# Layer 0's attention in pieces, with the order of four engines written out for seven heads

## The chip, the cores and the metric

The kernel runs on one core of a Trainium2 chip. The core has a matmul engine (PE, TensorE), a vector engine (DVE, VectorE), an activation engine (ACT, ScalarE), a general engine (POOL, GpSimd) and a queue that issues transfers (SP, SyncE). Each engine works through its own list of instructions in order and waits on semaphores of the others. The metric is the device time of one execution in microseconds (us), lower is better; the time before is the median of three runs.

## The reference

A trunk of two layers on 1024 positions of 1024 values in float32. Layer 0 mixes positions by differential attention, layer 1 by latent attention, and each is followed by a gated feed-forward block with a causal convolution. The change touches layer 0's attention: 8 heads, each with two score maps on 64 dimensions and one value map of 128.

```
q, k, v = split(h @ w_qkv)               # q, k: 8 heads x 2 maps x 64;  v: 8 heads x 128
q, k = rope on the first 16 of each 64
lam = exp(sum(lq1*lk1)) - exp(sum(lq2*lk2)) + lambda_init
sc = q k^T / 8                           # per head and map, keys up to the query's chunk of 64
p = softmax(sc)
a = p[map 0] - lam * p[map 1]
o = rms_norm(a @ v, subln_g) * (1 - lambda_init)
x = x + o @ w_o
```

## The kernel before

**Tiling.** Matrix products run in a reduced float32 format; to keep precision every operand is split into a high part (`hi`, a ScalarE cast) and a remainder (`lo`, a subtraction), and `mm3` (L116) issues three matmuls for a product, at lines 119 to 121. A head needs six projection units of 24 matmuls of 512 columns: keys, queries and values, for the first and the second half of the positions. They accumulate in a single PSUM bank, named `u`. A value sum is copied (L556) and then transposed; a key or query sum goes through a swap (L237) and a cosine product (L238) on VectorE, then two steps on GpSimd (L239, L240), then casts and remainders. The next unit can't start in bank `u` before its reader has finished.

**Steps.** `steps` (L281) runs 32 steps, t = 4 x head + p. Step p takes the query blocks 2p and 2p+1 (j = 0, 1; 128 rows each) against all keys up to their own. For each j: scores of both maps (L1622, L1623) into one of two double banks `S` (one holds both maps for p = 0 and 1, for p = 2 and 3 each map has its own), the mask and the maximum (L1626 to L1631), two exponentials with their sums (L1637), the reciprocal (L1647), the factor with lambda (L1648), the scaling of map 0 (`scale`: GpSimd L149 for p = 0 and 1, ScalarE L147 for p = 2 and 3) and the mix of the two maps (L1650). One step later the mixed weights are transposed in groups of up to four blocks of 128 (L252), split (`hi`, `lo`) and multiplied with the values; the product of 256 columns is copied (L1665). Every second step closes half a head's output: squares (L1668, L1669, remainder on GpSimd), their sum by two matmuls with ones (L1678, L1679), the root (`rsqrt`, L170) and a store by SP. Three banks `b` rotate among transposes, products and sums.

**Weights.** A head's three weight tiles are fetched by SP into two places in turn, split by ScalarE (1024 columns, `hi`) and GpSimd (`lo`, 1024 columns), and kept in four tiles. `prepare` (L515) does one split a step and fetches the next tile.

**What sets the order.** Before the steps a stretch is written out by hand (`manual_schedule`). The steps themselves are left to the framework's scheduler, which orders each engine by its own estimate of when things are ready; `steps` only gives it the program order: scores 0, projection piece, transposes of the step before, scaling and scores 1, the other projection pieces, products of the step before. Tiles that share a place make the later writer wait for the earlier readers.

## Time and profile before

| | us |
|---|---|
| median of 3 runs | 2427.79 (2427.32 to 2431.45) |
| profiled execution | 2430.68 |
| its span | 2428.9 |
| first scores of head 0 (from the span's start) | 48.12 |
| first scores of head 7 | 459.04 |

The profile shows one execution. Busy time is what an engine's instructions took; the idle time before an instruction is put down to the one that released it. In a row of instructions, "out<-in" names the tiles: `u<-s,s` on PE is a projection into bank u, `S<-u,h` and `S<-u,u` are scores, `b<-ident,u` transposes of the weights, `b<-u,u` products with the values. Casts are often printed at line 127 and remainders at line 130, the lines of `hi` and `lo`. DVE's idle time counts only where someone waits for DVE.

### The profile page before, as it was taken

The page shows a single profiled execution, that of the slowest core. Times are in us where ns is not written, and L with a number is a line of the kernel's source. Part 1 is how long each engine was busy: PE and PEld are TensorE (multiplying, and loading weights), DVE is VectorE, ACT ScalarE, POOL GpSimd, SP SyncE. Part 2 cuts the span into 40 slices and gives each one's busy share as a digit, 9 for nine tenths or more (in the row PEclk, how much of TensorE's full clock was granted, in tenths as well). Part 3 has the DMA queues.
Part 4 walks back from the last instruction along what each step waited for, and adds up shares of the span by engine and source line. Part 5 has one row for each costly group of instructions (what it writes and reads, how often), then busy time and mean ns, then how long its engine had stood idle before and what let it go on. Part 6 is the DMA issues. An engine that isn't in the chain of part 4 may idle for free.

```text
span 2428.9 us, 32660 instructions
## 1 busy us (share of the span) xinstructions
PE 2355.0 (97%) x11936; PEld 1997.5 (82%) x11936; DVE 1916.0 (79%) x3111; ACT 1305.3 (54%) x2446; POOL 618.5 (25%) x489
## 2 busy tenths in 40 slices
PE   7999999999999999999999999999999999999998
PEld 6888787887888888878899788988878888887886
DVE  6667776857888888889964777887488888888997
ACT  5677777755444444444445777776244444444444
POOL 4545454424100000000041666665330000000001
PEclk9999999999999999999999999999999999999999
DMA  4111111223322222554221211114322222227502
GB/s 161 40 35 44 35 35 44 100 93 100 99 82 79 87 78 88 187 175 131 72 103 46 77 40 29 49 59 134 96 87 87 79 87 87 78 86 278 172 3 78
DMA packets 95792, 213.91 MB, mean 88 GB/s; under 512 B 8720, under 2 KB 33936, under 8 KB 95632
## 3 DMA queue, kind: packets, MB, share of 16 engines
q1 hardware_dynamic: 86448, 184.04, 23.1%
q10 hardware_dynamic: 9184, 27.79, 3.1%
q8 instruction: 94, 1.54, 0.3%
q14 instruction: 66, 0.54, 0.1%
HBM read 159.37 MB, written 52.43 MB: 87 GB/s over the span
## 4 chain that ended last, share of the span: by engine, by line
PE 82%; DVE 7%; ACT 5%; DMA 3%; issue 2%; POOL 1%; SPq 0%; DVEq 0%; POOLq 0%; ACTq 0%
PE S L119 13%; PE S L121 13%; PE S L120 13%; PE b L119 8%; PE b L120 8%; PE b L121 8%; PE u L119 4%; PE u L120 4%; PE u L121 4%; PE b L252 3%; DMA u<-g_d 2%; PE u L1727 1%; DVE s L130 1%; PE u L1726 1%; ACT s L127 1%
## 5 line engine op out<-in xcount | busy, mean ns | idle before, releaser
L167 POOL TENSOR_TENSOR st<-st,mhalf 128x1 f32<-128x1 f32 x56 | 36.6, 654 | 1314.1 <-DVE st L164 1305.5
L127 ACT CAST u<-h 128x512 fp32r<-128x512 f32 (+2 forms) x242 | 145.9, 619 | 297.4 <-DVE h L847 277.7
L119 PE MATMUL S<-s,u 128*128 128x512 f32 (+1 forms) x768 | 290.5, 378 | 7.6 <-ACT s L127 2.6
L121 PE MATMUL S<-s,u 128*128 128x512 f32 (+1 forms) x768 | 289.5, 377 | 0.1
L120 PE MATMUL S<-s,u 128*128 128x512 f32 (+1 forms) x768 | 289.4, 377 | 0.0
L119 PE MATMUL b<-s,u 128*128 128x512 f32 x588 | 231.0, 393 | 1.5 <-DVE u L130 0.8
L121 PE MATMUL b<-s,u 128*128 128x512 f32 x588 | 229.3, 390 | 0.0
L120 PE MATMUL b<-s,u 128*128 128x512 f32 x588 | 229.2, 390 | 0.0
L904 DVE SCALAR_TENSOR_TENSOR u<-u,conv,u 128x1023 f32<-128x1023 f32 (+1 forms) x176 | 225.8, 1283 | 1.4 <-ACT u L900 1.4
L149 POOL TENSOR_TENSOR u<-u,st 128x384 f32<-128x384 f32 (+7 forms) x160 | 169.7, 1068 | 151.0 <-DVE st L1712 106.7
L127 ACT CAST s<-u 128x512 fp32r<-128x512 f32 (+2 forms) x230 | 145.0, 666 | 108.2 <-PE u L121 35.8
L119 PE MATMUL u<-s,s 128*128 128x512 f32 (+1 forms) x440 | 178.5, 406 | 13.4 <-ACT h L556 7.0
L130 DVE TENSOR_TENSOR u<-b,u 128x512 fp32r<-128x512 f32 (+1 forms) x256 | 157.4, 629 | 29.4 <-ACT u L127 28.0
L119 PEld LDWEIGHTS S<-s,u 128*128 128x128 f32 x768 | 145.2, 189 | 35.1 <-ACT s L127 5.5
L121 PE MATMUL u<-s,s 128*128 128x512 f32 (+1 forms) x440 | 173.2, 394 | 0.0
L120 PE MATMUL u<-s,s 128*128 128x512 f32 (+1 forms) x440 | 172.8, 393 | 0.0
L121 PEld LDWEIGHTS S<-s,u 128*128 128x128 f32 x768 | 145.2, 189 | 26.6 <-DVE u L130 0.5
L120 PEld LDWEIGHTS S<-s,u 128*128 128x128 f32 x768 | 145.3, 189 | 26.1
L130 DVE TENSOR_TENSOR s<-u,s 128x512 fp32r<-128x512 f32 (+2 forms) x210 | 150.0, 746 | 12.4 <-ACT s L127 12.2
L127 ACT CAST u<-b 128x512 fp32r<-128x512 f32 (+1 forms) x256 | 133.2, 550 | 37.9 <-PE b L252 28.9
L907 ACT ACTIVATE u<-u 128x1024 f32<-128x1024 f32 x44 | 46.7, 1062 | 187.5 <-DVE u L904 187.5
L130 DVE TENSOR_TENSOR u<-h,u 128x512 fp32r<-128x512 f32 x164 | 112.7, 687 | 32.5 <-ACT u L127 31.5
(270 smaller groups left out, 6561.1 us busy)
## 6 DMA issues: line engine op xcount, KB each, us to landing
u<-in_ffn_up SPq DMA_DIRECT2D x88, 512.0 KB, 3.9
g_d<-u ACTq DMA_DIRECT2D x44, 512.0 KB, 2.6
u<-in_ffn_down SPq DMA_DIRECT2D x66, 256.0 KB, 4.8
u<-g_d SPq DMA_DIRECT2D x62, 256.0 KB, 4.4
s<-in_da_wqkv SPq DMA_DIRECT2D x23, 512.0 KB, 3.6
x_d<-u SPq DMA_DIRECT2D x16, 512.0 KB, 2.9
s<-x_d SPq DMA_DIRECT2D x8, 1024.0 KB, 10.8
u<-o_d SPq DMA_DIRECT2D x24, 256.0 KB, 2.9
```

Source lines behind the costliest of these rows:

```text
L119: mm(out, lh, rl, start=first, stop=False, skip_group_check=onto)
L120: mm(out, lh, rh, start=False, stop=False, skip_group_check=onto)
L121: mm(out, ll, rh, start=False, stop=last, skip_group_check=onto)
L127: self.nc.scalar.copy(out, src)
L130: (eng or self.nc.vector).tensor_sub(out, src, hi.bitcast(F32))
L149: self.nc.gpsimd.tensor_mul(x, x, s.to_broadcast(list(x.shape)))
L167: nc.gpsimd.tensor_tensor(r, s, self.mhalf, ALU.pow)
L252: self.nc.tensor.transpose(ps[:, j * P : (j + 1) * P], probs[t][:, k : k + P], self.ident)
L904: nc.vector.scalar_tensor_tensor(t[half][:, back:], u[half][:, : S - back], w, t[half][:, back:], ALU.mult, ALU.add)
L907: nc.scalar.activation(t[0], t[0], AF.Silu)
L1726: nc.tensor.matmul(o[:, c0:], v, al, start=kb == 0, stop=False)
L1727: nc.tensor.matmul(o[:, c0:], v, ah, start=False, stop=kb == 2 * p + 1)
```

## The change

The work of a step is cut into some 45 named pieces, and a table with one row for each p says in which order they are issued, for steps 0 to 27 (heads 0 to 6) on PE, DVE, ACT and POOL (`da_steps`). A name without a mark belongs to the step itself, each `'` to one step earlier, `+` to the next. The letters: S scores, M mask and maximum, E exponential, I reciprocal and lambda product, C scaling, X mix, T transposes, H high part, L remainder, A product with the values, O its copy, Q squares, F their sum, R and N the root on ScalarE and VectorE, Wh and Wl the split of a weight tile. U and V are the step's projection units: 0 and 1 are the halves of its 24 matmuls, c the copy, t the transposes, h and l the split of values, s the swap, m the cosine, p and a the two GpSimd steps, ka to kd and qa to qf the casts and remainders of keys and queries. Head 7 keeps the old manner, with the same pieces called in a fixed sequence and then ordered by the scheduler.

```diff
+    DA_SCORE = (
+        "S0 S1 M0 Up O'' R2''' V0 X1' R3''' N1''' M1 T1' Ua E0a H1' L1' Uka E1a T0' H0' T2' Ukb Ukc V1 E0b L0' I0 E1b A0' N2''' T3'",
...
+    def da_steps(self, attend, units, prepare, n):
+        E = mybir.EngineType
+        region = ExitStack()
+        region.enter_context(self.tc.manual_schedule(engines={E.PE, E.DVE, E.Activation, E.Pool}))
+        steps, last = [], 28
+        for t in range(-1, n + 2):
...
+            if t == last:
+                region.close()
...
+            for name in self.DA_SCORE[t % 4].split():
+                step = t - name.count("'") + name.count("+")
+                if 0 <= step < min(n, last):
+                    steps[step](name.strip("+'"))
+            if t < last:
+                continue
...
```

A weight tile's fetch is now issued with the remainder that frees its place:

```diff
         def split_w(h, which):
...
+            def high():
+                st.raw = raws.pop((h, which))
+                st.w = self.w([P, 2, D], F32R)
+                heads[h]["w", which] = st.w[:, 0, :], st.w[:, 1, :]
+                self.hi(st.w[:, 0, :], st.raw)
+
+            def low():
+                self.lo(st.w[:, 1, :], st.raw, st.w[:, 0, :], nc.gpsimd)
+                fetch_w(*{1: (h, 2), 0: (h + 1, 1), 2: (h + 1, 0)}[which])
```

The lambda product moves from ScalarE to VectorE, and the root reads the sum's bank directly; its sign is turned, and the gain's with it:

```diff
-        nc.scalar.mul(w, l[:, 1:2], k.neglam)
+    def invert(self, j):
+        k.nc.vector.reciprocal(l, l)
+        k.nc.vector.tensor_scalar_mul(l[:, 1:2], l[:, 1:2], k.neglam)
...
-        nc.scalar.activation(v, x, AF.Identity, bias=self.eps, scale=scale)
-        nc.scalar.activation(t, v, AF.Ln)
+            act(self.tmp, self.ss, AF.Ln, bias=k.eps, scale=1.0 / P)
...
-        nc.vector.scalar_tensor_tensor(t, t, -0.5, v, ALU.mult, ALU.mult)
-        nc.vector.scalar_tensor_tensor(r, t, 1.5, r, ALU.add, ALU.mult)
+            stt(self.tmp, self.ss, EPS * P, self.tmp, ALU.add, ALU.mult)
+            stt(self.r, self.tmp, 1.5, self.r, ALU.subtract, ALU.mult)
```

What this moves is seen best at two places. The first is ScalarE around the copy of a value sum out of bank u, the first half of head 4. Before (the copy is the line 556; 174 and 175 are the root, 1637 exponentials, 1648 the lambda product, 147 a scaling, 1665 a product's copy):

```order
L1648 ACTIVATE st_519_2589<-st_509_2542,neglam 128x1
L147 ACTIVATE u_512_2557<-u_512_2557,st_509_2542 128x640
L127 CAST u_528_2632<-h_526_2626 64x512 x4
L1665 COPY h_500_2510<-b_2511 128x256
L174 ACTIVATE h_505_2528<-b_2524,eps 128x512
L127 CAST u_516_2579<-b_2574 128x512
L175 ACTIVATE h_506_2529<-h_505_2528 128x512
L556 COPY h_554_2758<-u_2685 128x512
L1637 ACTIVATE u_525_2612,st_521_2595<-S_2597,st_520_2594 128x768
```

The same place now (the copy is the line 635; 1820 exponentials, 1869 a product's copy, 1875 and 1878 squares):

```order
L1869 COPY h_475_2508<-b_2540 128x256
L127 CAST u_495_2622<-h_487_2574 64x512
L1878 ACTIVATE h_501_2666<-h_475_2508 128x512
L1875 ACTIVATE h_502_2668<-h_475_2508 128x512
L635 COPY h_503_2672<-u_2605 128x512
L127 CAST u_505_2679<-b_2661 128x512
L127 CAST u_506_2681<-b_2674 128x512
L127 CAST u_507_2683<-b_2657 128x384
L1820 ACTIVATE u_510_2692,st_509_2691<-S_2631,st_498_2654 128x896
```

The root's two steps and a cast are gone from the place ahead of the copy, the squares stand there instead, and the casts of the transposes and the exponentials of p = 3 come behind it.

The second place is GpSimd from the scalings of p = 0 to the query remainders of the second half. Before (149 scalings, 239 and 240 the rotary steps, 130 remainders: 1024 columns are a weight tile, 64x512 queries, `h<-h,h` squares):

```order
L149 TENSOR_TENSOR u_568_2821<-u_568_2821,st_566_2813 128x128
L130 TENSOR_TENSOR s_679_3392<-s_54_146,s_679_3392 128x1024
L239 TENSOR_TENSOR h_609_3046<-h_609_3046,s_53_145 128x512
L130 TENSOR_TENSOR s_622_3122<-s_54_146,s_622_3122 128x1024
L240 TENSOR_TENSOR h_608_3045<-h_608_3045,h_609_3046 128x512
L149 TENSOR_TENSOR u_582_2882<-u_582_2882,st_580_2874 128x256
L149 TENSOR_TENSOR u_599_2993<-u_599_2993,st_597_2985 128x384
L130 TENSOR_TENSOR h_57_149<-h_608_3045,u_610_3051 64x512
L130 TENSOR_TENSOR h_58_150<-h_608_3045,u_610_3051 64x512
```

Now (684 are the rotary steps):

```order
L149 TENSOR_TENSOR u_536_2830<-u_536_2830,st_535_2829 128x128
L130 TENSOR_TENSOR s_518_2750<-s_54_146,s_518_2750 128x1024
L149 TENSOR_TENSOR u_540_2838<-u_540_2838,st_539_2837 128x256
L149 TENSOR_TENSOR u_552_2910<-u_552_2910,st_551_2909 128x384
L130 TENSOR_TENSOR s_554_2933<-s_54_146,s_554_2933 128x1024
L130 TENSOR_TENSOR h_563_2990<-h_560_2982,h_556_2951 128x512
L684 TENSOR_TENSOR h_558_2976<-h_558_2976,s_53_145 128x512
L684 TENSOR_TENSOR h_565_2996<-h_565_2996,h_558_2976 128x512
L149 TENSOR_TENSOR u_570_3007<-u_570_3007,st_569_3006 128x512
L130 TENSOR_TENSOR h_57_149<-h_565_2996,u_573_3033 64x512
L130 TENSOR_TENSOR h_58_150<-h_565_2996,u_573_3033 64x512
```

All four scalings, both weight remainders and the squares' remainder now stand ahead of the query remainders, which the scores of p = 2 read.

## The prediction

> **What bounds the kernel now.** The page's first part and its chain of waits come first.

> ```profile
> PE 2355.0 (97%) x11936; PEld 1997.5 (82%) x11936; DVE 1916.0 (79%) x3111; ACT 1305.3 (54%) x2446; POOL 618.5 (25%) x489
> PE 82%; DVE 7%; ACT 5%; DMA 3%; issue 2%; POOL 1%; SPq 0%; DVEq 0%; POOLq 0%; ACTq 0%
> ```

> TensorE is busy 97% of the span and holds 82% of the chain, so the change can win only where TensorE stands still within the stage that it touches. That stage runs from the first score matmul of head 0 (48.12 us) to that of head 7 (459.04 us). The table by stretches of time has it, then two of its heads, and behind it the rest of the last head and the later attention of layer 1; its columns are length, then busy time of PE, PEld, DVE, ACT and POOL.

> ```profile
> 48.12:459.04 410.92, 391.41 (x2080) 331.79 (x2081) 295.91 (x518) 293.87 (x616) 212.27 (x150) 0.99 0.13 43
> 221.22:280.49 59.27, 56.20 (x303) 47.58 (x302) 42.10 (x75) 40.87 (x88) 29.48 (x21) 1.00 0.11 36
> 280.49:336.50 56.01, 54.64 (x301) 46.83 (x301) 43.06 (x74) 43.63 (x92) 30.31 (x21) 1.00 0.12 38
> 459.04:500.00 40.96, 40.76 (x236) 35.47 (x235) 34.35 (x63) 34.01 (x77) 16.90 (x14) 1.00 0.31 103
> 1360.00:1680.00 320.00, 313.87 (x2042) 280.51 (x2042) 260.96 (x635) 238.89 (x527) 207.66 (x165) 1.00 0.17 50
> ```

> In seven heads TensorE is idle 410.92 - 391.41 = 19.5 us, 2.8 us a head. No other engine is near its limit: VectorE 296, ScalarE 294, GpSimd 212 of 411 us. So 19.5 us is the most that a better order can win there. Who is waited for, with total, times and longest, between 48.12 and 459.04 us:

> ```profile
> PE u L119 <- ACT h L556: 7.0, 6, 1.3
> PE S L1622 <- ACT u L1637: 6.6, 5, 1.5
> PE u L119 <- DVE h L238: 4.3, 5, 1.4
> PE S L1622 <- POOL h L130: 1.1, 2, 0.6
> PE b L186 <- DVE u L130: 0.9, 3, 0.3
> ```

> These add to 19.9 us (two waits straddle the window's edge), so the loss has names. 11.3 us of it is the single accumulator bank u: a projection can't begin until the one before has been copied (L556, values) or rotated (L238, keys and queries). 6.6 us is the two score banks S, held until the exponentials (L1637) have read them. One of the waits in order of time:

> ```profile
> 258.98 0.69 ACT L174 ACTIVATE h<-b,eps 128x512 f32<-128x512 f32 x1
> 259.57 0.58 ACT L127 CAST u<-b 128x512 fp32r<-128x512 f32 x1
> 260.03 0.64 ACT L175 ACTIVATE h<-h 128x512 f32<-128x512 f32 x1
> 260.56 0.58 ACT L556 COPY h<-u 128x512 f32<-128x512 f32 x1
> 257.19 0.60 PE L252 MATMUL b<-ident,u 128*128 128x128 f32 x4
> 257.54 0.48 PE L1622 MATMUL S<-u,h 128*128 128x512 f32 x1
> 259.15 0.40 PE L121 MATMUL u<-s,s 128*128 128x512 f32 x1
> 259.38 0.49 PE L252 MATMUL b<-ident,u 128*128 128x128 f32 x3
> 261.20 0.50 PE L119 MATMUL u<-s,s 128*128 128x512 f32 x1 [1.33 <-ACT h L556]
> ```

> The value sum is complete near 259.5 us. ScalarE has root and cast pieces queued ahead of its copy, which ends at 261.1; TensorE had 0.3 us of transposes as cover and loses 1.33 us. This is order, not load.

> **Is 19.5 us the room?** TensorE's busy time has modelled ends, so I look inside a projection. From its second to its 24th matmul:

> ```profile
> 51.68 0.40 PE L120 MATMUL u<-s,s 128*128 128x512 f32 x1
> 56.69 0.39 PE L121 MATMUL u<-s,s 128*128 128x512 f32 x1
> L120 PEld LDWEIGHTS u<-s,s 128*128 128x128 f32 x372 | 70.8, 190 | 12.7
> ```

> 5.01 us over 22 steps is 0.228 us a matmul, against 0.19 us for its weight load, so the columns set the pace and no order changes that. [...]

> **The change, part by part.** Every piece of the seven heads is now placed by hand on all four engines; instructions on TensorE stay the same in number and size.

> Lambda product to VectorE: 56 ScalarE instructions of 0.305 us go, 56 of about 0.15 us on VectorE come. The root without a copy: 14 of 0.69 us go from ScalarE (the row at 258.98 is one), and one VectorE step now reads PSUM, 0.68 instead of 0.69 us by the nearest row. The sums' bank is held longer in return, until that step. Both engines are free a quarter of the time: 0 us by themselves. Without that cover the copy is the 0.6 us ahead of L556 above, at most 7 x 1.2 us, and this lies inside the 19.5.

> ```profile
> L1648 ACT ACTIVATE st<-st,neglam 128x1 f32<-128x1 f32 x56 | 16.8, 305 | 18.0 <-DVE st L1647 17.8
> L229 DVE TENSOR_SCALAR neglam<-neglam 128x1 f32<-128x1 f32 x1 | 0.2, 154 | 0.0
> L130 DVE TENSOR_TENSOR u<-b,u 128x512 fp32r<-128x512 f32 x54 | 35.8, 681 | 12.2 <-ACT u L127 11.6
> L178 DVE SCALAR_TENSOR_TENSOR h<-h,h 128x512 f32<-128x512 f32 x12 | 8.2, 685 | 1.3 <-ACT h L177 1.2
> ```

> The bank u. Half a projection is 12 x 0.228 = 2.73 us. In the new table the copy of value half 0 (Uc) is followed on TensorE by 11 transposes before the next use of the bank, about 1 us by the row of four (257.19 to 257.54), against a copy of 0.58 us: a margin of 0.4 us. Value half 1 (Vc', first on ScalarE in row 1) has 0.6 + 0.35 + 0.8 + 0.7 = 2.4 us of cover. For keys and queries the swap and the cosine take 1.35 us and have at least one group of scores, transposes or products ahead. I take 11.3 us of waits down to 1 to 3.

> The banks S. Between the last scores of p=2 and the first of p=3 stand one product group (0.6) and half a projection (2.73): 3.4 us. Under it lie two maxima of 0.95 us, the later exponential (0.9 + 0.2) and a 0.1 us memset: 3.1 us plus handovers. Margin 0 to 0.3, so 6.6 us falls to 0 to 3.

> The port. Row p=1 is where a new wait may come. Here VectorE and GpSimd exclude each other:

> ```profile
> 226.29 2.46 POOL L130 TENSOR_TENSOR s<-s,s 128x1024 fp32r<-128x1024 f32 x1 [5.08 <-ACT s L127]
> 226.42 3.41 DVE L1650 SCALAR_TENSOR_TENSOR u<-u,st,u 128x1024 f32<-128x1024 f32 x1
> 168.71 1.27 DVE L1650 SCALAR_TENSOR_TENSOR u<-u,st,u 128x1024 f32<-128x1024 f32 x1
> L130 POOL TENSOR_TENSOR s<-s,s 128x1024 fp32r<-128x1024 f32 x22 | 53.0, 2408 | 48.0 <-ACT s L127 33.7 <-issue 12.0 <-DVE st L1647 1.8
> L130 POOL TENSOR_TENSOR h<-h,u 64x512 fp32r<-64x512 f32 x29 | 40.5, 1396 | 14.4 <-PE b L121 7.4 <-ACT u L127 5.9
> L240 POOL TENSOR_TENSOR h<-h,h 128x512 f32<-128x512 f32 x29 | 39.0, 1346 | 1.1 <-DVE st L1647 0.5
> L149 POOL TENSOR_TENSOR u<-u,st 128x512 f32<-128x512 f32 x7 | 7.3, 1044 | 9.5 <-DVE st L1647 9.5
> L149 POOL TENSOR_TENSOR u<-u,st 128x128 f32<-128x128 f32 x7 | 2.8, 399 | 22.5 <-DVE st L1647 22.4
> 345.95 0.34 DVE L1650 SCALAR_TENSOR_TENSOR u<-u,st 128x128 f32<-128x128 f32 x1
> 64.36 0.73 DVE L1650 SCALAR_TENSOR_TENSOR u<-u,st 128x512 f32<-128x512 f32 x1
> ```

> The mix of 1024 columns takes 1.27 us alone and 3.41 us when a weight remainder (2.4 us) holds the port. From the end of row 0 to the first scores of p=2 the table gives GpSimd: four scalings (0.4 to 1.04, in all 2.9), two weight remainders (4.8), one square's remainder and two rotary steps (3 x 1.3), two query remainders (2.8): 14.4 us. VectorE's steps with both operands in SBUF there are four mixes (0.34 to 0.73, 2.2), a key remainder (0.7), two root steps (1.4): 4.3 us. That is 18.7 us through one port. TensorE's own work in that stretch is four half projections (10.9), five product groups (3.3), scores (1.7), 20 transposes (1.9), the sums (0.5): 18.3 us. The two are equal, and the last GpSimd piece, the query remainders, is what the scores of p=2 wait for. So 0.4 us is lost if the port never rests, 1.5 us if it rests once for a scaling that waits for its reciprocal (22.5 + 9.5 us of idle over 14 scalings is 2.3 us each today, with far less queued behind). I take 0.7 us.

> Queues. SP issues the same fetches and stores. A weight fetch now follows its remainder on GpSimd and is needed at the earliest a row later, over 12 us, against 3.6 us to landing; a store's tile is wanted again for the square's remainder about 4 us after, against 2.0 us. Nothing there.

> ```profile
> s<-in_da_wqkv SPq DMA_DIRECT2D x23, 512.0 KB, 3.6
> o_d<-h SPq DMA_DIRECT2D x16, 256.0 KB, 2.0
> ```

> Behind the table. Head 7 is left to the scheduler; TensorE idles only 0.2 us there, so it can only lose, at most what an average head idles now, 2.8 us. The order of layer 1's attention moves too; it idles 6.1 us in 320, I allow 3 us either way and take 0.

> **The sum.** Idle left a head: 0.3 at u, 0.1 at S, 0.7 at the port, 1.1 us; times 7 is 7.7. Win 19.5 - 7.7 = 11.8 us. The profiled execution took 2430.68 us (span 2428.9 and 1.8 around it), which gives 2418.9; it lies 2.9 us above the median of the runs, 2427.79, and from that the forecast is 2416.0 us. With the waits' bounds (0.4 to 2.3 us a head: the port's 0.4 and nothing else, or 1.5 with 0.4 each at u and S) the win is 16.7 to 3.4 us, and with the 3 us behind this case spans 2408 to 2427.

> **The rivals.**
> All idle vanishes: the margins hold in every head and the port's work runs beside. 19.5 us less, 2408.3. For it: three engines have a quarter free. Against: margins of 0 to 0.4 us in three places a head.

> The win is given back: head 7 starts with the table's leftovers and the layer 1 order falls badly, 2.8 and 3 us lost, the waits at their upper bound (2.3 x 7 = 16.1): 19.5 - 16.1 - 5.8, about 2 us slower, 2430, no measurable difference. That the table misses the waits altogether gives the same time.

> Slower, by the port: in row 1 both engines now have a fixed order, so whoever loses the port blocks all behind it. A key remainder that loses to a weight remainder holds up the maximum queued behind it on VectorE, and with it exponentials and scalings, while the port then rests. If each of the three scalings that follow a reciprocal waits 1.3 us with the port idle, row 1 is 18.7 + 3.9 = 22.6 us against 18.3: 4.3 us a head, 30 us in seven, 10.6 more than is won, 2438. It decides from 2.8 us of port idle a head. [...]

> **How the numbers follow.** Forecast 0.54, all idle gone 0.12, given back 0.13, slower 0.21. A difference under 0.2%, 4.9 us, can't be told from none; the forecast's end above 2422.9 lies in it, for which I set 0.05 of its 0.54. Faster: 0.49 + 0.12 = 0.61; same: 0.05 + 0.13 = 0.18; slower: 0.21. The range takes in the forecast's span and most of the first rival (with 3 us more from layer 1 it would reach 2405), so 2406, and above it goes half the way from 2427 to 2438, to 2433, past the second rival.

> **What would show it.** Right: TensorE's idle time in the seven heads falls to 5 to 11 us; the waits for L556's copy and for L1637 are nearly gone; the largest left is a score matmul of p=2 or the sums waiting for GpSimd. Wrong: idle time above 19.5 us there, with scalings or weight remainders as releasers (port), or a stage that is shorter while head 7 or layer 1 grew (given back). More matmul time at the same count would mean that the pace of 0.228 us was no floor.

## The result: 0.33% slower

| | before | after |
|---|---|---|
| median of 6 runs, us | 2428.88 (2426.72 to 2431.45) | 2437.90 (2436.89 to 2439.16) |
| span of the profiled execution, us | 2428.9 | 2436.8 |

The ratio is 1.0033, with a 95% interval of 1.0023 to 1.0042: 9 us slower, where 2416.0 was forecast. The first part of the page of the changed kernel and its chain of waits hardly differ from those of before; TensorE is busy 97% of a longer span.

```profile
PE 2362.0 (97%) x11936; PEld 2003.5 (82%) x11936; DVE 1960.8 (80%) x3175; ACT 1290.5 (53%) x2366; POOL 623.7 (26%) x489
PE 81%; DVE 8%; ACT 4%; DMA 3%; POOL 2%; issue 2%; SPq 0%; POOLq 0%; ACTq 0%; DVEq 0%
```

So the page has to be cut into stages. TensorE's order is the same instruction for instruction from the 3000th matmul to the 6500th (the output projection and the first feed-forward block) and again from the 8500th on, so the times of these matmuls are fair marks; head 0's and head 7's first scores are two more. First the changed kernel, then the stages of before that the prediction doesn't show (columns: length, then busy time of PE, PEld, DVE, ACT, POOL, the granted clock, DMA):

```profile
46.80:448.40 401.60, 390.19 (x2088) 332.35 (x2087) 338.89 (x572) 280.18 (x548) 219.20 (x151) 0.99 0.14 45
448.40:589.90 141.50, 132.03 (x681) 110.44 (x680) 90.89 (x145) 76.03 (x146) 45.45 (x40) 0.98 0.32 103
1340.30:1670.60 330.30, 316.81 (x2002) 280.66 (x2001) 262.28 (x624) 243.08 (x523) 211.64 (x165) 0.98 0.17 51
1670.60:2426.90 756.30, 746.83 (x3437) 622.02 (x3436) 619.78 (x881) 329.85 (x532) 66.25 (x54) 1.00 0.30 101
```
```profile
459.04:592.50 133.46, 130.50 (x686) 110.17 (x685) 89.99 (x134) 78.92 (x159) 46.03 (x40) 1.00 0.33 109
1343.50:1665.60 322.10, 312.80 (x2002) 277.39 (x2001) 261.42 (x624) 241.70 (x524) 212.26 (x165) 0.99 0.18 52
1665.60:2419.00 753.40, 744.06 (x3437) 619.70 (x3436) 619.86 (x881) 330.06 (x532) 65.22 (x54) 1.00 0.31 102
```

| stage | before | after | difference |
|---|---|---|---|
| up to head 0's first scores | 48.1 | 46.8 | -1.3 |
| seven heads, to head 7's first scores | 410.9 | 401.6 | -9.3 |
| head 7 and first part of the projection, to the 3000th matmul | 133.5 | 141.5 | +8.0 |
| 3000th to 6500th matmul | 751.0 | 750.4 | -0.6 |
| layer 1's attention, to the 8500th | 322.1 | 330.3 | +8.2 |
| the rest | 753.4 | 756.3 | +2.9 |

The seven heads won 9.3 us, and 19 us were lost behind them: in head 7, which the diff leaves to the scheduler, and in stages that it doesn't touch. In the steady heads 1 to 5 the forecast's picture holds: of the waits listed before, for L556, L238 and L1637, none recurs, and in each of these heads TensorE stops twice, for a remainder and for the sums that wait for GpSimd (two heads, then the stops between 103 and 394 us with total, times and longest):

```profile
102.00:157.83 55.83, 55.08 (x302) 47.16 (x302) 48.00 (x84) 40.36 (x80) 30.42 (x22) 1.00 0.12 38
157.83:213.66 55.83, 55.09 (x302) 47.16 (x302) 47.97 (x84) 40.35 (x80) 30.42 (x22) 1.00 0.11 38
```
```profile
PE b L1886 <- POOL h L130: 2.1, 5, 0.4
PE b L119 <- DVE u L130: 1.6, 5, 0.3
```

A head takes 55.83 us, against (59.27 + 56.01) / 2 = 57.64 before. Three places come next; the first of them, the seam, lies ahead of head 7's first scores, so that its loss is inside the 9.3 us of the heads.

**The seam to head 7.** Timeline of the changed kernel, TensorE, VectorE, ScalarE, GpSimd:

```profile
429.72 1.31 PE L1841 MATMUL b<-ident,u 128*128 128x128 f32 x10 [3.92 <-DVE u L1833]
424.26 5.41 DVE L1833 SCALAR_TENSOR_TENSOR u<-u,st,u 128x768 f32<-128x768 f32 x1 [1.45 <-ACT u L147]
422.33 1.05 ACT L127 CAST s<-s 128x1024 fp32r<-128x1024 f32 x1
422.44 2.88 POOL L130 TENSOR_TENSOR h<-h,u 64x512 fp32r<-64x512 f32 x2 [2.46 <-issue]
425.29 2.34 POOL L130 TENSOR_TENSOR s<-s,s 128x1024 fp32r<-128x1024 f32 x1
427.60 1.25 POOL L130 TENSOR_TENSOR h<-h,h 128x512 fp32r<-128x512 f32 x1
```

The mix of 768 columns ends only after GpSimd's pieces of 2.88, 2.34 and 1.25 us have gone by, and TensorE stops 3.92 us. The cast and the 2.34 us are not in the table: they split the first output weight, fetched ahead for the projection, and the scheduler has put them among the rows of the table. One head earlier, with neither, the mix slips in between the two query remainders (VectorE, GpSimd):

```profile
367.46 1.47 DVE L1833 SCALAR_TENSOR_TENSOR u<-u,st,u 128x768 f32<-128x768 f32 x1 [0.50 <-ACT u L147]
366.60 3.49 POOL L130 TENSOR_TENSOR h<-h,u 64x512 fp32r<-64x512 f32 x2 [2.45 <-issue]
```

**The projection.** Its second token tile needs head 7's last output, by way of DRAM (ScalarE at the end of the sums, VectorE, SP, ScalarE, TensorE):

```profile
528.54 0.69 ACT L1893 ACTIVATE h<-b,eps 128x512 f32<-128x512 f32 x1 [3.94 <-PE b L1887]
532.11 0.75 DVE L1906 SCALAR_TENSOR_TENSOR h<-h,g_sub,h 128x512 f32<-128x512 f32 x1
532.89 0.33 SPq L1907 DMA_DIRECT2D o_d<-h  x1
535.17 7.10 SPq L728 DMA_DIRECT2D u<-o_d  x3
538.68 0.62 ACT L127 CAST h<-u 128x512 fp32r<-128x512 f32 x1 [2.78 <-DMA u<-o_d]
539.35 0.79 PE L119 MATMUL S<-s,h 128*128 128x512 f32 x1 [5.89 <-ACT h L127]
```

From the sums to the product are some 11 us. But TensorE now does head 7's last sums 40 matmuls later among the projection's (they begin with matmul 2729, before with 2689), so that the products that covered this way before are spent already.

**Layer 1's attention.** The scheduler gives it another order, though nothing there is edited. By the rows above TensorE is idle there for 13.5 us where it was for 9.3, which is half of the 8.2 us; two more stretches of half clock (below) account for at most 3.4 more. TensorE's largest waits between 1430 and 1680 us, of the changed kernel and of before:

```profile
PE b L252 <- DVE u L130: 4.6, 8, 0.8
PE S L119 <- ACT u L1930: 2.5, 1, 2.5
PE b L252 <- DVE S L1928: 1.2, 1, 1.2
```
```profile
PE b L252 <- DVE u L130: 1.6, 3, 0.8
PE S L119 <- ACT u L1706: 1.3, 4, 0.5
```

**The clock.** The stop of 5.89 us costs more than its length. Behind it TensorE runs at half clock, with 9 matmuls in 4.45 us where 16 follow in 3.40 (the granted clock is the third column from the right):

```profile
539.35:543.80 4.45, 4.31 (x9) 2.98 (x10) 1.28 (x1) 0.00 (x0) 3.01 (x3) 0.50 0.27 75
543.80:547.20 3.40, 3.40 (x16) 2.77 (x15) 0.00 (x0) 0.00 (x0) 0.00 (x0) 1.00 0.22 61
```

Up to the last matmul each such stretch lasts 3.41 or 6.83 us in the two profiles. Before has 13.7 us of them, half of which, 6.8 us, is lost at most; after has ten times 3.41 us, 17.1 lost at most. At most, because a stretch can begin within the stop: the 6.83 us at the projection start at 536.95 us, 2.4 us before TensorE goes on, and by the 4.31 us of busy time in the row they lose 2.2 us and not 3.4. The last stage differs by the clock alone: TensorE's idle time is 9.3 and 9.5 us there, with two more stretches of half clock. One of them does not go by the stop's length, as a stop of 2.60 us stands at that matmul in both kernels (at 1786.3 us before, at 1792.6 now) and half clock follows only in the changed one.

### The profile page after: what moved, and what is told of

It is laid out like the page before. It is cut to its first block, busy times and chain, and to the rows that moved or that the text cites. A ratio compares the mean times of both kernels' runs of the same rounds, so it can differ in the third digit from the quotient of the medians.

```text
span 2436.8 us, 32572 instructions
## 1 busy us (share of the span) xinstructions
PE 2362.0 (97%) x11936; PEld 2003.5 (82%) x11936; DVE 1960.8 (80%) x3175; ACT 1290.5 (53%) x2366; POOL 623.7 (26%) x489
## 4 chain that ended last, share of the span: by engine, by line
PE 81%; DVE 8%; ACT 4%; DMA 3%; POOL 2%; issue 2%; SPq 0%; POOLq 0%; ACTq 0%; DVEq 0%
PE S L121 13%; PE S L119 13%; PE S L120 13%; PE b L121 8%; PE b L120 8%; PE b L119 8%; PE u L119 4%; PE u L120 4%; PE u L121 4%; PE b L252 2%; DVE s L130 1%; ACT s L127 1%; PE u L1951 1%; PE S L1794 1%; PE u L1950 1%
## 5 line engine op out<-in xcount | busy, mean ns | idle before, releaser
L119 PE MATMUL S<-s,u 128*128 128x512 f32 (+1 forms) x768 | 291.0, 379 | 7.2 <-DVE u L1081 3.7
L127 ACT CAST u<-h 128x512 fp32r<-128x512 f32 (+2 forms) x242 | 145.8, 619 | 279.9 <-DVE h L987 278.9
L121 PE MATMUL S<-s,u 128*128 128x512 f32 (+1 forms) x768 | 290.0, 378 | 0.1
L120 PE MATMUL S<-s,u 128*128 128x512 f32 (+1 forms) x768 | 289.9, 378 | 0.0
L119 PE MATMUL b<-s,u 128*128 128x512 f32 x588 | 230.6, 392 | 0.5
L121 PE MATMUL b<-s,u 128*128 128x512 f32 x588 | 229.1, 390 | 0.0
L120 PE MATMUL b<-s,u 128*128 128x512 f32 x588 | 228.9, 389 | 0.0
L149 POOL TENSOR_TENSOR u<-u,st 128x384 f32<-128x384 f32 (+7 forms) x160 | 172.4, 1084 | 183.5 <-DVE st L1936 113.5
L127 ACT CAST s<-u 128x512 fp32r<-128x512 f32 (+2 forms) x230 | 144.9, 665 | 117.1 <-PE u L121 36.0
L119 PE MATMUL u<-s,s 128*128 128x512 f32 (+1 forms) x440 | 177.1, 403 | 4.1 <-DVE h L656 2.9
L127 ACT CAST u<-b 128x512 fp32r<-128x512 f32 (+1 forms) x256 | 134.5, 547 | 77.6 <-PE b L1841 35.3
L130 DVE TENSOR_TENSOR u<-b,u 128x512 fp32r<-128x512 f32 (+1 forms) x256 | 159.0, 633 | 20.0 <-ACT u L127 17.2
L119 PEld LDWEIGHTS S<-s,u 128*128 128x128 f32 x768 | 145.9, 190 | 35.0 <-ACT s L127 4.1
L120 PE MATMUL u<-s,s 128*128 128x512 f32 (+1 forms) x440 | 172.6, 392 | 0.0
L121 PE MATMUL u<-s,s 128*128 128x512 f32 (+1 forms) x440 | 172.3, 392 | 0.0
L121 PEld LDWEIGHTS S<-s,u 128*128 128x128 f32 x768 | 146.0, 190 | 26.6 <-DVE u L130 0.5
L120 PEld LDWEIGHTS S<-s,u 128*128 128x128 f32 x768 | 146.0, 190 | 26.1
L130 DVE TENSOR_TENSOR s<-u,s 128x512 fp32r<-128x512 f32 (+2 forms) x210 | 151.3, 754 | 17.9 <-ACT s L127 17.7
L130 DVE TENSOR_TENSOR u<-h,u 128x512 fp32r<-128x512 f32 x164 | 112.7, 687 | 32.6 <-ACT u L127 31.5
## 6 DMA issues: line engine op xcount, KB each, us to landing
u<-in_ffn_up SPq DMA_DIRECT2D x88, 512.0 KB, 4.0
g_d<-u ACTq DMA_DIRECT2D x44, 512.0 KB, 2.6
u<-in_ffn_down SPq DMA_DIRECT2D x66, 256.0 KB, 5.1
u<-g_d SPq DMA_DIRECT2D x62, 256.0 KB, 4.3
s<-in_da_wqkv SPq DMA_DIRECT2D x23, 512.0 KB, 3.7
x_d<-u SPq DMA_DIRECT2D x16, 512.0 KB, 2.9
u<-o_d SPq DMA_DIRECT2D x24, 256.0 KB, 3.0
```

The source lines that it names most:

```text
L119: mm(out, lh, rl, start=first, stop=False, skip_group_check=onto)
L120: mm(out, lh, rh, start=False, stop=False, skip_group_check=onto)
L121: mm(out, ll, rh, start=False, stop=last, skip_group_check=onto)
L127: self.nc.scalar.copy(out, src)
L130: (eng or self.nc.vector).tensor_sub(out, src, hi.bitcast(F32))
L149: self.nc.gpsimd.tensor_mul(x, x, s.to_broadcast(list(x.shape)))
```

## The experiments

Theory A: the table wins its 12 us, and the seam, the projection and layer 1's order give it back, each with half clock behind its stops. Rivals: denser work lowers the clock by itself (B), the arithmetic edits cost (C), a stop that is removed reappears elsewhere (D). All medians here go with a kernel before between 2428.9 and 2430.6 us on the same chip; they come from three chips.

**e1, the output weights' places.**

```diff
-prefetcher(a["da_w_o"], W, slots(*range(8)), units(10, 11, 12, 13))
+prefetcher(a["da_w_o"], W, slots(1, 0, 2, 3, 4, 5, 6, 7), units(10, 11, 12, 13))
```

> The change, with one edit: the four output weights that are fetched and split ahead during the last heads take their places in the order 1, 0, 2, 3 instead of 0, 1, 2, 3. Place 1 comes free half a projection later, so that the first weight remainder on GpSimd (2.34 us, at 425.29 in the change) now comes after the square's remainder of head 6 instead of before it. The same instructions otherwise; as a side effect the scheduler's order of layer 1's attention on TensorE becomes that of the kernel before. Theory A (the table wins its 12 us, and three things behind it give it back: the port at the seam to head 7, the projection that waits for head 7's output, layer 1's order; each stop of 1.5 us or more also halves TensorE's clock for 3.4 us): the stop of 3.93 us at 425.8 falls to under 1 us and its half-clock stretch goes, 3 + 1.7 = 4.7 us, and layer 1 gives back some 7 us: 2438 - 4.7 - 7 = 2426 us, about 3 us faster than before; the stop of 5.9 us at 533 stays. Theory B (denser work lowers the granted clock, wherever it stops; the half-clock stretches are spread by the power drawn and not by the stops): the clock's loss stays near 17 us, the time at 2433 to 2438. Theory C (the arithmetic edits cost the time): 2436 to 2438.

**e2 and e3, the short way for head 7's last output**, in the load of the projection (e3 with `scalar.copy`):

```diff
-        self.nc.sync.dma_start(o, o_d[ks[0] : ks[0] + 4, :, s].rearrange("k p s -> p k s"))
+        short = self.ends is not None and i == 4 and ks[0] == 4
+        self.nc.sync.dma_start(o[:, : 4 - short, :], o_d[ks[0] : ks[0] + 4 - short, :, s].rearrange("k p s -> p k s"))
+        if short:
+            self.nc.vector.tensor_copy(o[:, 3, :], self.ends[:, :P])
+            self.ends = None
```

> The change, with one edit: of the one load of the output projection that waits for head 7's last store (token tile 4, heads 4 to 7), head 7's quarter is copied by VectorE from the tile on the chip instead of taking the way through DRAM (store 2.0 us, load 3.5 us). Layer 1 keeps the order of the change. Theory A: the stop of 5.89 us at 533.5 falls by about 5 us to under 1 us, and the 6.8 us at half clock behind it (3.4 us lost) go too: 2438 - 8.5 = 2429.5 us, no difference from before. Theory B: the stop may go, the clock's loss stays: 2433. Rival D (the stop is hidden anyway or only moves: the next load, for token tile 5, waits for the same store): 2436 to 2438.

> As e2_tail_vector, with the small copy on ScalarE instead of VectorE. The heads and the projection are the same to the instruction on TensorE; behind them the scheduler gives layer 1's attention the order of the kernel before (six matmuls apart) instead of that of the change. So the difference from e2_tail_vector prices layer 1's order alone. Theory A: 7 us less than e2_tail_vector, 2422.5 us, 6 us faster than before. If layer 1's order is worth nothing and its loss in the change comes from the clock or from what stands ahead of it: the same as e2_tail_vector, within 2 us.

**e4, both edits** (e1 and e2).

> Both edits, the weights' places (e1) and the short way for head 7's quarter on VectorE (e2); layer 1 has the order of the change. Theory A: 2438 - 4.7 - 8.5 = 2425 us; with e1 it prices the projection's stop and layer 1's order against each other (e1 lacks the first, has the second). Theory B: 2433. Theory C: 2436 to 2438.

**e5 and e6, layer 1's order by a dead copy**: e5 adds it to e4, e6 to the change itself.

```diff
             def root():
                 st.r = k.root(st.s, D)
+                if i == 1:
+                    nc.vector.tensor_copy(k.stat(), st.r)
```

> e4_both and one dead instruction: at the end of layer 0's second part, VectorE copies a 128x1 statistic that nobody reads (about 0.15 us). Nothing else is edited, but behind it the scheduler gives layer 1's attention the order of the kernel before, from its 1000th matmul on to the last. Theory A (layer 1's order costs the change 8 to 10 us, as e2 against e3 has it): 2428 - 8 = 2420 us, 9 us faster than the kernel before, by a ratio of 0.996. If the 9 us between e2 and e3 were the copy engine's and not the order's: 2428.

> The change, and the same dead copy alone: both stops behind the table stay (3.9 us at the seam, 5.9 us at the projection), layer 1's attention has the order of the kernel before but for its first 500 matmuls. Theory A: 2438 - 8 = 2430 us, no difference from before, which would make layer 1's order the greatest of the three losses. If the order is free: 2438.

Measured, with the ratio to the kernel before (for layer 1, "of before" is its order from about the 7000th matmul on in e1 and e3, from the 7500th in e5 and e6):

| | us | ratio, 95% | seam's stop | projection's stop | layer 1's order |
|---|---|---|---|---|---|
| the change | 2437.9 | 1.0023 to 1.0042 | 3.9 | 5.9 | its own |
| e2 | 2433.8 | 1.0009 to 1.0027 | 3.9 | 1.0 | its own |
| e6 | 2430.8 | 0.9998 to 1.0017 | 3.9 | 5.9 | of before |
| e4 | 2428.0 | 0.9987 to 1.0005 | 1.3 | 1.0 | its own |
| e1 | 2424.7 | 0.9969 to 0.9988 | 1.3 | 5.9 | of before |
| e3 | 2424.5 | 0.9968 to 0.9986 | 3.9 | 1.0 | of before |
| e5 | 2419.6 | 0.9947 to 0.9976 | 1.3 | 1.0 | of before |

The rows price each place twice. The projection's stop: 2437.9 - 2433.8 = 4.1 and, e1 against e5, 5.1 us. The seam's: e2 against e4 5.8, e6 against e1 6.1. Layer 1's order: e2 against e3 9.3, e4 against e5 8.4, the change against e6 7.1. One price of each, 4.6 + 5.9 + 8.3 = 18.8, leads from the change to 2419.1, where e5 is, so the three add up and hardly touch each other. With each kernel taken against the one before on its own chip, none of these prices moves by more than 0.5 us. Theory A holds, with the projection's price half of what it expected; C would leave all these kernels near 2437 and falls. So does D, as no longer stop follows where one was removed. e5 (four executions) beats both kernels, by 0.39% the one before; the granted clock of its profiled execution is 0.995, that of before 0.996, so not every loss is gone from it.

What the edits did is seen in the trace. In e1 the weight's remainder comes behind the square's, and the stop falls from 3.92 to 1.26 us, where under 1 was expected (TensorE, VectorE, GpSimd):

```profile
427.08 1.09 PE L1841 MATMUL b<-ident,u 128*128 128x128 f32 x8 [1.26 <-DVE u L1833]
425.00 2.03 DVE L1833 SCALAR_TENSOR_TENSOR u<-u,st,u 128x768 f32<-128x768 f32 x1
427.11 1.28 POOL L130 TENSOR_TENSOR h<-h,h 128x512 fp32r<-128x512 f32 x1 [0.89 <-POOL h L130]
428.47 2.42 POOL L130 TENSOR_TENSOR s<-s,s 128x1024 fp32r<-128x1024 f32 x1
```

In e2 (its lines stand one to six further down) the cast waits for a copy on the chip instead of a load (VectorE, TensorE). A second stop of 0.63 us follows for the remainder, so that 4.2 us of the stop are won; one stretch of half clock stays (from 535.1 to 538.5 us a matmul every 0.43 us, before and behind it every 0.23) and loses 1.7 us, where the two of the change had lost 2.2 and not the 3.4 that I had counted. This is why 4.1 us were won and not 8.5:

```profile
532.14 0.23 DVE L732 COPY u<-h 128x128 f32<-128x128 f32 x1
533.75 0.50 PE L120 MATMUL S<-s,h 128*128 128x512 f32 x1 [1.04 <-ACT h L128]
535.12 0.60 PE L122 MATMUL S<-s,h 128*128 128x512 f32 x1 [0.63 <-POOL h L131]
```

e2 and e3 differ by the engine of one copy of 0.2 us, but layer 1 takes 329.3 us in the one and 321.3 in the other:

```profile
1336.29:1665.60 329.31, 315.24 (x2001) 279.23 (x2001) 262.54 (x624) 243.19 (x523) 212.01 (x165) 0.99 0.17 51
```
```profile
1337.90:1659.20 321.30, 311.64 (x2002) 277.41 (x2001) 261.60 (x624) 242.13 (x523) 212.36 (x165) 0.99 0.17 52
```

TensorE stands still 14.1 us there in e2 and 9.7 in e3; the rest of the 8 us is busy time, one more stretch of half clock (between 1600 and 1660 us the granted clock is 0.97 in e2 and 1.00 in e3) and some 2 us that I can't name. Theory B falls too: in e4, as dense in the heads as the change, at most 8.5 us are lost to half clock instead of 17.1 (granted clock of the profiled execution: 0.995 instead of 0.992). Five stretches are gone: three stood behind the two stops that were removed, the other two, in the change, behind stops of 2.02 us at 63 us and of 2.09 us at 2227 us.

**e7, the arithmetic edits alone**, in the kernel before (the lambda product and the root, as in the diff above, no table).

> The kernel before with the two arithmetic edits alone (lambda product on VectorE, root without a copy), its heads left to the scheduler, no table. The scheduler gives other orders in the heads, and in layer 1 the order of the change. Theory A: nothing in the heads (within 3 us, by another order), 8 us lost in layer 1, in all 2434 to 2440. Theory C (the arithmetic itself costs: more work on VectorE, the sums' bank held longer): the heads' stage of 411 us longer by 5 us or more. If neither counts: 2429.

**e8, three heads by the table**: `last = 12` for `last = 28`.

> The change with three heads by the table instead of seven; heads 3 to 7 are left to the scheduler. Layer 1 keeps the order of the change; the last sums stand 24 matmuls (5.5 us) earlier among the projection's. Theory A: four heads lose 1.8 us each, 7.3 us, by the 2000th matmul; the seam's stop (3 us over the usual, and 1.7 of clock) and the projection's (5.5 and 3.4) go: 2438 + 7.3 - 4.7 - 8.9 = 2432 us. Theory B (denser order lowers the clock) would have less clock lost with fewer heads by the table, all through. Rival E (the table's win isn't 1.8 us a head, but was made in head 0 alone): the 2000th matmul at 382 us as in the change.

e7 took 2431.4 us (0.9998 to 1.0017), e8 2429.3 (0.9995 to 1.0014). e8's total is near what theory A had (2432): with four heads out of the table its 2000th matmul is at 389.6 us, in the change at 381.8, which is 8 us later, and yet the kernel is 8.6 us faster, since from there to the 3000th it takes 12.0 us less. But the first scores of the heads show where the 8 us are. Head 2, the last one in e8's table, takes 62.80 us where it takes 55.84 in the change; heads 3 to 5, left to the scheduler, take 166.7 us together, against 167.5 by the table. So the loss is at the table's end, wherever that stands (head 6 takes 62.8 us in e1, e4 and e5, with the seam's stop repaired), and four scheduled heads do not lose 1.8 us each. e7 was a surprise: it reached the 3000th matmul at 584.0 us, before at 592.5 and the change at 589.9. Either the arithmetic that I had put at nothing wins in the heads, or the other order that the scheduler made for it does. e9 to e12 go after this.

**e9, the table with the old arithmetic.**

```diff
-        k.nc.vector.tensor_scalar_mul(l[:, 1:2], l[:, 1:2], k.neglam)
+        k.nc.scalar.mul(l[:, 1:2], l[:, 1:2], k.neglam)
...
-            act(self.tmp, self.ss, AF.Ln, bias=k.eps, scale=1.0 / P)
+            act(self.v, self.ss, AF.Identity, bias=k.eps, scale=1.0 / P)
+            act(self.tmp, self.v, AF.Ln)
```

> The change with its two arithmetic edits undone and the table kept: the lambda product back on ScalarE (0.3 us each), the root again by way of a copy of the sums (0.7 us more of ScalarE), in the same places of the same order. TensorE's order in the heads is that of the change up to its 2000th matmul; layer 1 gets the order of the kernel before. If the arithmetic is hidden under the table: 279 us from the 500th to the 2000th matmul as in the change, and in all 2438 - 8 (layer 1) = 2430 us, less what the seam's and the projection's stops happen to change. If the arithmetic and not the order made the win in the heads (the kernel before with these edits alone reached the 3000th matmul 5 us earlier, net of half clock): 282 to 285 us in that stretch, in all 2433 to 2436.

**e10** is e7 with the dead copy, **e11** the kernel before with the lambda product alone on VectorE, **e12** with the root alone without its copy.

> The kernel before with the two arithmetic edits and no table (e7), and the dead copy that gives layer 1 the order of the kernel before. It says what the table is worth when both have the better order in layer 1 and neither has long stops at the seam and the projection. If layer 1's order is again worth 8 us: 2431.4 - 8 = 2423.4 us, against 2419.6 for the table with both repairs: the table itself is then worth 4 us in 2420. If the order is worth less here: 2427 to 2431, and the table more.

> The kernel before with the lambda product on VectorE alone: 56 instructions of 0.3 us go from ScalarE and 56 of 0.2 us come to VectorE, and the scheduler reorders the heads, and gives layer 1 the order of the change. If the arithmetic edits help in themselves (e7 gained 5 us in the heads): some 2 to 3 us by the 3000th matmul for each of the two. If it was the luck of another order: anything from -5 to +3 us there. Behind it layer 1's order costs 7 to 8: 2432 to 2438 in all.

> The kernel before with the root's copy gone alone (14 copies of 0.69 us from ScalarE). The scheduler reorders the heads, and layer 1 keeps exactly the order of the kernel before. If the arithmetic helps in itself: 2 to 3 us less by the 3000th matmul, 2426 to 2427 in all; if ScalarE's load is hidden there: 2429; if the order decides, up to 5 us either way.

| | us | ratio, 95% | at the 3000th matmul, less half clock |
|---|---|---|---|
| before | 2428.9 | | 589.1 |
| e9, table, old arithmetic | 2432.7 | 0.9998 to 1.0016 | 590.3 |
| e7, both edits, no table | 2431.4 | 0.9998 to 1.0017 | 584.0 |
| e10, as e7, other order in layer 1 | 2424.5 | 0.9967 to 0.9987 | 583.2 |
| e11, lambda alone | 2432.7 | 1.0002 to 1.0021 | 583.6 |
| e12, root alone | 2425.4 | 0.9972 to 0.9991 | 580.4 |
| e5, both edits, table, both repairs | 2419.6 | 0.9947 to 0.9976 | 578.2 |

e9 is beyond both expectations: from the 500th to the 2000th matmul it takes 288.8 us where the change takes 279.2 with the same order on TensorE. (In all it is still faster than the change: it has layer 1's order of before, and no stop at the seam.) Two heads of before, one of e9, and two of e7:

```profile
221.22:336.50 115.28, 110.83 (x602) 94.42 (x601) 85.16 (x148) 84.50 (x179) 59.79 (x42) 1.00 0.11 37
```
```profile
101.50:159.25 57.75, 55.64 (x302) 47.10 (x301) 45.96 (x75) 43.54 (x90) 29.52 (x22) 1.00 0.11 37
```
```profile
129.10:242.20 113.10, 110.64 (x602) 94.03 (x601) 87.77 (x166) 79.22 (x159) 58.25 (x43) 1.00 0.12 38
```

Per head: 57.64 before, 57.75 with the table and the old arithmetic, 56.55 with the new arithmetic and the scheduler's order, 55.83 with both. With the old arithmetic the table wins nothing. With the new it is 0.7 us a head ahead of e7, but that is one order of the scheduler's: e12, with the root alone and no table, takes 278.6 us from head 1's first scores to head 6's, 55.7 a head, and the scheduled heads 3 to 5 of e8 take 55.6. So the order that the scheduler happens to make is worth as much as the 0.7, and that the table orders these heads better than the scheduler isn't shown. What the old arithmetic costs under the table is seen in TensorE's waits between 103 and 390 us of e9, in five heads, and in time on ScalarE and TensorE:

```profile
PE u L119 <- DVE h L652: 3.1, 5, 0.6
PE u L119 <- ACT h L635: 3.0, 5, 0.6
```
```profile
143.23 0.29 ACT L1826 ACTIVATE st<-st,neglam 128x1 f32<-128x1 f32 x1 [0.62 <-DVE st L1825]
144.69 0.94 ACT L147 ACTIVATE u<-u,st 128x768 f32<-128x768 f32 x1
148.26 0.56 ACT L635 COPY h<-u 128x512 f32<-128x512 f32 x1
148.88 0.50 PE L119 MATMUL u<-s,s 128*128 128x512 f32 x1 [0.60 <-ACT h L635]
```

The lambda product stands in ScalarE's fixed row and waits 0.62 us for VectorE's reciprocal; everything behind it moves, down to the copy of bank u, and TensorE waits 0.60 us for that copy, in every head. In the change the same copy comes 1.52 us earlier, of which 0.5 us were there already at the projection ahead, and nothing waits for it:

```profile
146.74 0.56 ACT L635 COPY h<-u 128x512 f32<-128x512 f32 x1
147.47 0.48 PE L119 MATMUL u<-s,s 128*128 128x512 f32 x1
```

The other wait, as long and for the swap (L652), belongs to the root (VectorE, TensorE in e9):

```profile
128.24 1.77 DVE L1903 SCALAR_TENSOR_TENSOR h<-h,h 128x512 f32<-128x512 f32 x1
131.32 0.50 PE L119 MATMUL u<-s,s 128*128 128x512 f32 x1 [0.62 <-DVE h L652]
```

With the copy this step reads both operands on SBUF and takes 1.77 us here; the wait behind it comes once in every head. Without the copy it reads the sum's bank and takes 0.68 us at the same place in the change (128.08), all of it under a GpSimd remainder (127.68 to 129.30). That GpSimd is what holds it up in e9 is my reading, from the root of the kernel before: a step of the same size with both operands on SBUF (L179) takes 0.69 us at 223.98, where GpSimd rests, and 1.67 at 202.10, under a remainder that runs from 201.55 to 203.22. The rotation's steps stand behind it, and TensorE waits for the swap. The two waits make 1.2 of the 1.9 us that a head loses; what each edit is worth alone under the table was not run. The old arithmetic is not load that hides: it is waits in front of steps that TensorE needs.

e10 shows layer 1's order once more (2431.35 - 2424.54 = 6.8 us, or 8.5 with each taken against the kernel before on its own chip). e11 and e12 don't split the two edits cleanly: each moves the scheduler's order in the heads, and both come out faster there, by 5.5 and 8.7 us, more than I had expected of either, and e12 with half of the edits by more than e7 with both. What the table with its repairs is worth beside the arithmetic stays open: e5 is 5 us ahead of e10, 3 with each against its own chip's kernel before, and the two intervals overlap.

## Why the prediction was wrong

- **What bounds, and how much idle there is to win** was right: the seven heads are TensorE's, and the pace of 0.228 us a matmul stayed (in the change 0.23 from 147.79 to 149.86 us; 390.19 us of matmul time for 2088 of them, before 391.41 for 2080). Idle time there fell from 19.5 to 401.60 - 390.19 = 11.4 us; without the seam's stop it is 7.5, and 7.7 was forecast. That these two agree is in part luck: a steady head idles 0.75 us where I had put 1.1, and head 0 adds two waits of 2.5 us together that I had not.
- **Bank u and the banks S** went as reckoned, to nothing but for these two waits in head 0, behind the cosine product. **The port** in row 1 costs 0.4 us a head (the sums' wait), the lower end of my bounds. The slower rival, 30 us by the port in row 1, did not come; that its 2438 is the measured time is luck. What the port did cost was one place between rows, the seam, 5.9 us, which I had not looked at. There it went as in the rival, the engine that came second blocked and all behind it: VectorE's mix, begun at 424.26 under GpSimd's second query remainder, ended 0.82 us after the last of GpSimd's three pieces (429.67 against 428.85) and took 5.41 us, where it took 1.47 a head earlier.
- **"Both engines are free a quarter of the time: 0 us by themselves"** failed. By e9 against the change the arithmetic is worth 1.9 us a head under the table. The total for the heads, 9.3 us with the seam and some 15 with it repaired (e4: 395.6 us against 410.9) where 11.8 was forecast, rested on the wrong part of the change: an engine's free share says nothing of an instruction that waits in the middle of its order. My own bound without cover, 7 x 1.2 us for the copy, had left out this wait, and the root's step that I had put at 0.68 instead of 0.69 us is 0.68 instead of 1.77 at one of its two places.
- **"Behind the table: head 7 can lose at most 2.8 us, layer 1 3 us either way, I take 0"** is the step that turned the sign. From head 7's first scores to the 3000th matmul the change loses 8.0 us, of which the projection's stop is 4.6, and layer 1's order costs 7 to 9 by four pairs of kernels. The rival "the win is given back" had the right place, and its sign came true, a stage that is shorter while head 7 and layer 1 grew; but its prices of 2.8 and 3.0 are a third of the measured 8.0 and 8.2. I priced each stage by the idle time of before, but what bounds the loss there is not the idle time: it is the cover that a wait loses (11 us from head 7's sums to its product, hidden before) and the half clock.
- **The clock** was in no term. The profile of before showed it: 0.99 in the row of the seven heads, from one stretch of 6.8 us that begins at 449.2 us, behind a stop of 1.46 us (446.2) and within one of 1.44 (448.9).
- **Queues: nothing there** held in the heads. But SP's round trip through DRAM at the end of head 7 was not looked at, because the diff leaves its instructions as they are.

## What to carry to other kernels

Where a scheduler orders what lies behind an edit, a change wins in its own stage and draws a new order in the others: compare stage by stage at marks with the same order, and try the edit with two or three meaningless variations before judging it, since here one dead copy was worth 7 to 8 us. The same holds for judging an order written by hand: compare it with more than one order of the scheduler, since here these differed by as much as the hand's win. A path that is covered today, such as the last store and load between two stages, needs its own line in a forecast: how long it is, and what will cover it when everything ahead gets denser. Count an instruction that waits for another engine by its wait, also on an engine with time to spare.
